# A hybrid attention/S5 layer on one core: the in-projection keeps its split weights in DRAM, and the FFN's silu becomes one ScalarE instruction

## The chip, the core and the metric

The kernel runs on one core of a Trainium2 chip. The engines that matter here are TensorE (PE: matmuls, with PEld for its weight loads), VectorE (DVE), ScalarE (ACT), GpSimd (POOL) and SyncE (SP), which issues most DMAs. Each engine works through its own instructions in order. A DMA issued by an engine stands in that engine's instruction order: if it has to wait for a buffer, everything behind it on that engine waits too. The metric is device time in microseconds (us), the median of several runs; lower is better.

## The reference, cut to what matters

One layer over 2048 latent tokens of width 1024 with 256 context tokens, all in fp32:

```python
n_lat = modulate(rmsnorm(h, attn_norm_g), sh1, sc1)          # and n_ctx of the context
q, k, v, u, gate_attn, gate_ssm = split(n_lat @ w_in)         # 512,512,512,512,1024,1024 columns
a = neighbourhood_attention(rope(q), rope(k), v, k_ctx, v_ctx, rpb)   # 8x16 window + context keys
s = s5_branch(u_ctx, u)                                       # two-way complex diagonal scan
h = h + g1 * ((sigmoid(gate_attn) * (a @ w_branch_attn) + sigmoid(gate_ssm) * (s @ w_branch_ssm)) @ w_out)
n = modulate(rmsnorm(h, ffn_norm_g), sh2, sc2)
a, b = split(n @ w_ffn_in)                                    # 2 x 2816 columns
h = h + g2 * ((silu(a) * b) @ w_ffn_out)
out = rmsnorm(h, final_norm_g)
```

## The kernel before, in words

**Three matmuls for one.** A product of fp32 numbers is made of fp32r matmuls: each operand is split in a high part (ACT cast, L70) and a low part (DVE subtract, L71), and `mm3` (L89 to L94) adds high·high, high·low and low·high in PSUM. Activations are kept split; weights are split when they are loaded.

**Weight pieces.** `piece` (L79) brings one piece of a weight matrix, 512 KB, 128 x 1024 numbers: `raw` (L73) takes one of two raw buffers and has SP load it (L76), then `split` writes `whi` and `wlo`, of which there are three buffers each. `cols` (L96) runs 24 matmuls of 512 columns with each piece (eight contraction steps, three matmuls each). `rows` (L111), for v, takes two pieces at a time, 96 matmuls of 256 columns, and both pieces are in use until the last tokens.

**The in-projection** (`in_proj`, L350) has four token blocks of 512 tokens. Each block goes through the same 28 pieces: 4 of k, 4 of v (two pairs), 4 of q (`w_qk`, `w_vu`), 16 gate pieces (`w_gate`). So each piece is loaded and split four times. Block 0 has its normalized tokens in SBUF already; blocks 1 to 3 load them at L357 (`n<-ns`) into a ring of 12 buffers. In block 1 the same ring serves `biases` (L430), which builds the attention's bias tables for eight heads on POOL: load (`n<-in_rpb`), compute (L442, L443), store (`bi<-n`, `be<-n`).

**What stands beside it.** `run` (L1211) emits the S5 scan (`s5`, L629, in sub-blocks whose tokens POOL loads at L651, `ut<-us`) first, the in-projection with a lower priority, and the attention between them; the program's scheduler merges them into one fixed order for each engine. So the pieces fill PE behind the S5's and the attention's own steps. SP's order also holds the outputs of q and k (`qs<-qt`, L368), the S5's strip loads (`mt<-strip`, L725, sixteen at a time) and its outputs (`ys<-yt`, L800).

**The FFN** (`ffn`, L1104) takes the four token blocks again. `ffn_in` makes each pair of hidden tiles with a seven-product scheme (Strassen) from weights whose sums POOL makes and which ACT and DVE split (L70, L71); DVE adds the products (L1085 to L1098). The silu of the first half is

```python
nc.scalar.activation(t, a, AF.Tanh, scale=0.5)
V.scalar_tensor_tensor(t, t, 1.0, a, op0=ALU.add, op1=ALU.mult)
```

that is, (1 + tanh(a/2))·a on ACT and DVE, and the missing factor one half is in the gate `g` (L228). Then DVE multiplies by the second half (L1137) and the result is split (`zh`, `zl`).

Of the kernel before, what the change touches and what calls it, by code (L numbers as in the profile page):

```python
# [10 lines left out]
F32 = mybir.dt.float32  # L11
F32R = mybir.dt.float32r
BF16 = mybir.dt.bfloat16
AF = mybir.ActivationFunctionType
ALU = mybir.AluOpType
# [3 lines left out]
P = 128  # L19
D = 1024  # L20
KD = D // P
# [31 lines left out]
class Kernel:  # L53
# [22 lines left out]
        self.nc.sync.dma_start(raw.rearrange("p k f -> p (k f)"), src[r, c])  # L76
        return raw

    def piece(self, src, r, c, nr):  # L79

        raw = self.raw(src, r, c, nr)
        with self.hot():
            hi = self.wh.tile([P, nr, 1024 // nr], F32R, name="whi")
            lo = self.wh.tile([P, nr, 1024 // nr], F32R, name="wlo")
            self.split(hi, lo, raw)
        next(self.between, None)
        return hi, lo

    def mm3(self, ps, l, r, first, last):  # L89

# [2 lines left out]
        mm(ps, l[0], r[1], start=False, stop=False)  # L93
        mm(ps, l[1], r[0], start=False, stop=last)  # L94

    def cols(self, pool, src, kt, c0, n, ops, tag="ps"):  # L96

        nm = 8 // kt  # L100
        for c in range(n):
            w = self.piece(src, 0, c0 + c, kt)
            for m in range(nm):
                sl = slice(m * P, (m + 1) * P)
                for i, (nt, f) in enumerate(ops):
                    ps = pool.tile([P, nt], F32, name=tag)
                    for k in range(kt):
                        self.mm3(ps, (w[0][:, k, sl], w[1][:, k, sl]), f(k), k == 0, k == kt - 1)
                    yield c * nm + m, i, ps

    def rows(self, pool, src, c, ops, tag="ps"):  # L111


        w = [self.piece(src, r, c, 4) for r in range(2)]
        for i in range(0, len(ops), 2):
            ps = pool.tile([P, 2, 256], F32, name=tag)
            for j in range(2):
                for k in range(KD):
                    self.mm3(ps[:, j], ops[i + j](k), (w[k // 4][0][:, k % 4], w[k // 4][1][:, k % 4]), k == 0, k == KD - 1)
            yield i, ps  # L120
# [6 lines left out]
    def constants(self):  # L127
        nc = self.nc
        self.cst = self.pool("cst")
        self.dr = self.pool("dr", space=DRAM)  # L130
        self.wr = self.pool("wr", 2)
        self.wh = self.pool("wh", 3)
        self.ident = self.cst.tile([P, P], F32, name="ident")
        make_identity(nc, self.ident)
        self.am = self.cst.tile([P, 92], F32, name="am")
        nc.sync.dma_start(self.am, self.I["amask"])
        self.ones = self.cst.tile([P, P], F32, name="ones")
        nc.vector.memset(self.ones, 1.0)
        self.mhalf = self.cst.tile([P, 4], F32, name="mhalf")
        nc.gpsimd.memset(self.mhalf, -0.5)  # L140
        self.hq = self.cst.tile([P, 4, NB, 4], F32, name="hq")
        d = self.dr
        self.qs = d.tile([2, 4, 2, 2, 32, L], F32, name="qs")
        self.ks = d.tile([2, 4, 2, 2, 32, LA], F32, name="ks")
        self.vs = d.tile([2, 32, 40, AW], F32, name="vs")
        self.vc = d.tile([LC, AW], F32, name="vc")
        self.bi = d.tile([H * 2, P, 440], F32, name="bi")
        self.be = d.tile([2, H * 2, P, 320], F32, name="be")
        self.us = d.tile([LA, AW], F32, name="us")
        self.ns = d.tile([NB, KD, P, 2, TB], F32, name="ns")  # L150
        self.gsc = d.tile([2, KD, NB, P, TB], F32, name="gsc")
        self.hs = d.tile([L, D], F32, name="hs")
        self.sums = d.tile([NHT, P, 2, 512], F32, name="sums")
        self.ysc = d.tile([4, P, 2, L], F32, name="ys")
        self.asc = d.tile([NB, 4, P, 2, TB], F32, name="as")
# [52 lines left out]
    def modulation2(self, tp, pp):  # L208


        nc, I = self.nc, self.I
        V = nc.vector
        for sec in (2, 3, 4, 5):
            for c2 in range(2):
                acc = tp.tile([P, 512], F32, name="macc")
                nc.gpsimd.memset(acc, 0.0)
                nc.sync.dma_start(acc[0:1], I["b_mod"][sec * D + c2 * 512:sec * D + c2 * 512 + 512].unsqueeze(0))
                for k0 in range(0, KD, 2):
                    w = self.raw(I["w_m2"], k0 // 2, (sec - 2) * 2 + c2, 2)
                    with self.hot():  # L220
                        for k in range(2):
                            V.scalar_tensor_tensor(acc, w[:, k], self.s2[:, k0 + k, 0:1], acc, op0=ALU.mult, op1=ALU.add)
                    yield
                if sec in (2, 5):
                    pg = pp.tile([P, 512], F32, name="ps")
                    nc.tensor.matmul(pg, self.ones, acc, start=True, stop=True)
                    with self.hot():
                        V.tensor_scalar(self.g[sec // 5][:, c2 * 512:c2 * 512 + 512], pg, 0.5, None, op0=ALU.mult)  # L228
                else:
                    pm = pp.tile([P, 4, 2], F32, name="ps")  # L230
                    for m in range(4):
                        nc.tensor.matmul(pm[:, m, :], acc[:, m * P:(m + 1) * P], self.ones[:, 0:2], start=True, stop=True)
                    cs = slice(c2 * 4, c2 * 4 + 4)
                    with self.hot():
                        if sec == 3:
                            V.tensor_copy(self.B[:, 2, cs], pm[:, :, 0])
                        else:
                            V.scalar_tensor_tensor(self.A[:, 2, cs], pm[:, :, 0], 1.0, self.ng[:, 1, cs], op0=ALU.add, op1=ALU.mult)
# [111 lines left out]
    def in_proj(self, ring, ev, pm, nt, nct):  # L350
        nc, I = self.nc, self.I
        V = nc.vector
        for b in range(NB):
            if b:
                nt = [ring.tile([P, 2, TB], F32R, name="n") for _ in range(KD)]
                for k in range(KD):
                    nc.sync.dma_start(nt[k].bitcast(F32), self.ns[b, k])  # L357
            t0 = b * TB
            cs = ev.tile([P, 2, TB], F32, name="cs", bufs=1)
            nc.sync.dma_start(cs, I["rope"][:, :, t0:t0 + TB])  # L360
            lat = (TB, lambda k, nt=nt: (nt[k][:, 0], nt[k][:, 1]))
# [6 lines left out]
                        nc.sync.dma_start(dst[:, j, d, h, :, t:t + n].rearrange("i r t -> r i t"), x[p:p + 32].bitcast(F32))  # L368

            def qk(c0, ops, isk):  # L370
                for jj, i, ps in self.cols(pm, I["w_qk"], KD, c0, 4, ops):
                    with self.hot():
                        qt = ev.tile([P, 2, TB], F32R, name="qt")
                        if i:
# [29 lines left out]
            for c in range(2):  # L404
                ops = [lambda k, j=j, nt=nt: tuple(nt[k][:, i, j * P:(j + 1) * P] for i in range(2)) for j in range(4)]
                if b == 0:
                    ops += [lambda k, j=j: tuple(nct[k // 2][:, k % 2, i, j * P:(j + 1) * P] for i in range(2)) for j in range(2)]
                oc = slice(c * 256, c * 256 + 256)
                for i, ps in self.rows(pm, I["w_vu"], c, ops):
                    e = ev.tile([P, 2, 256], F32, name="e")  # L410
                    with self.hot():
                        nc.scalar.copy(e, ps)
                    if i == 4:
                        nc.scalar.dma_start(self.vc[:, oc].rearrange("(j p) f -> p j f", p=P), e)
                        continue
                    row = (t0 + i * P) // 64
                    for r in range(2):
                        for hf in range(2):
                            nc.scalar.dma_start(self.vs[hf, row + r:row + 4:2, :, oc].rearrange("j c f -> c j f"),
                                              e[r * 64 + hf * 24:r * 64 + hf * 24 + 40])  # L420
            qk(0, [lat], False)
            for gi in range(2):
                for m, _, ps in self.cols(pm, I["w_gate"], KD, gi * 8, 8, [lat]):
                    g = ev.tile([P, TB], F32, name="e")
                    with self.hot():
                        nc.scalar.activation(g, ps, AF.Tanh, scale=0.5)
                    nc.scalar.dma_start(self.gsc[gi, m, b], g)
# [598 lines left out]
    def ffn_in(self, ch, b, X, pm, os, tp, up):  # L1026
# [32 lines left out]
        ops = []  # L1059
        for x in src:  # L1060
            with self.hot():
                hi = self.wh.tile([P, x.shape[1], 4, P], F32R, name="whi")
                lo = self.wh.tile([P, x.shape[1], 4, P], F32R, name="wlo")
                self.split(hi.rearrange("p a k m -> p a (k m)"), lo.rearrange("p a k m -> p a (k m)"), x)
            ops += [(hi[:, i], lo[:, i]) for i in range(x.shape[1])]
        s1, s3, s2, s4, a11, a22, a12 = ops
# [37 lines left out]
    def ffn(self, xs_, os, xp, tp, pm, first):  # L1104
        nc, I = self.nc, self.I
        V = nc.vector
        with ExitStack() as ctx:
# [13 lines left out]
            for b in range(NB):  # L1121
# [4 lines left out]
                for g, (p0, p1) in enumerate(groups):  # L1126
                    last = g == len(groups) - 1
                    zs = {}
                    for m2 in range(p0, p1):
                        ts = []  # L1130
                        for a in self.ffn_in(m2, b, X, pm, os, wp, up):
                            t = wp.tile([P, TB], F32, name="n")
                            nc.scalar.activation(t, a, AF.Tanh, scale=0.5)
                            V.scalar_tensor_tensor(t, t, 1.0, a, op0=ALU.add, op1=ALU.mult)
                            ts.append(t)
                        for m, a in enumerate(self.ffn_in(NHT // 2 + m2, b, X, pm, os, wp, up)):
                            V.tensor_tensor(ts[m], ts[m], a, op=ALU.mult)  # L1137
# [216 lines left out]
```

## Time and profile before

| | before |
|---|---|
| median of 3 runs | 3211.07 us (3209.65 to 3219.78) |
| the profiled execution's own time | 3210.19 us |
| its span in the trace | 3208.4 us |
| granted TensorE clock, mean | 0.987 |
| PE busy | 3088.2 us, 96% |
| DVE busy | 2340.6 us, 73% |
| ACT busy | 1567.5 us, 49% |
| POOL busy | 899.4 us, 28% |
| HBM read and written | 446.95 MB and 111.61 MB |

The time beside the span is what lies before and after the recorded instructions, 1.8 us. PE is busy nearly throughout, so time can be won only where PE is idle, and it is lost where something new makes it wait; the table says nothing on where that is. Block 0 of the in-projection ends at about 394 us, block 1 at 629, block 2 at 832, block 3 at 1045; the FFN begins at about 1740.

### The profile page before, as it was taken

To read this page: it belongs to the slowest core of one execution; us is meant where nothing else is said; L and a number is where in the kernel's file an instruction comes from. 1 tells how busy PE (TensorE), PEld (TensorE's weight loads), DVE (VectorE), ACT (ScalarE), POOL (GpSimd) and SP (SyncE) were. 2 spreads that over 40 slices of the span, in tenths; PEclk is the share of its full clock that TensorE was granted. 3 is DMA by queue.
4 is the path that set the end of the run, shared out by engine and by line. 5 is a ranking of instruction groups with operands and counts; after the bars stand their busy time and mean duration, and the time that the engine had idled before them with its cause. 6 is when DMAs were issued, how large, how long until landed. Compare 5 with 4: busy or idle time off the path is not lost.

```text
span 3208.4 us, 54284 instructions
## 1 busy us (share of the span) xinstructions
PE 3088.2 (96%) x20600; PEld 2716.4 (85%) x20600; DVE 2340.6 (73%) x4153; ACT 1567.5 (49%) x2746; POOL 899.4 (28%) x856
## 2 busy tenths in 40 slices
PE   7999978999999899999999999999999999999998
PEld 5988766787788788788888998989989998989988
DVE  6689787897753576665657866987868966886766
ACT  4545434454355556466554543454535543554534
POOL 2000053000223232222300544742242423341243
PEclk9999999999999999999999999999999999999999
DMA  8545467454676898887947434434434433443332
GB/s 320 187 126 170 162 195 239 170 163 143 205 242 186 268 277 241 254 250 223 267 152 248 141 122 139 148 129 134 133 128 150 135 112 125 148 145 128 116 109 102
DMA packets 212852, 564.27 MB, mean 176 GB/s; under 512 B 31784, under 2 KB 63656, under 8 KB 212592
## 3 DMA queue, kind: packets, MB, share of 16 engines
q1 hardware_dynamic: 155008, 437.48, 41.4%
q0 software_dynamic: 28032, 87.64, 10.1%
q10 hardware_dynamic: 29552, 35.70, 3.3%
q8 instruction: 162, 2.65, 0.3%
q14 instruction: 98, 0.80, 0.1%
HBM read 446.95 MB, written 111.61 MB: 174 GB/s over the span
## 4 chain that ended last, share of the span: by engine, by line
PE 74%; DVE 10%; DMA 10%; issue 3%; POOL 2%; ACT 1%; SPq 0%; ACTq 0%; POOLq 0%; DVEq 0%
PE ps L92 14%; PE ps L93 14%; PE ps L94 14%; PE ps L1075 8%; PE ps L1073 7%; PE ps L1074 7%; DVE wlo L71 3%; PE o L924 2%; DMA n<-in_rpb 2%; PE w L905 1%; PE w L884 1%; PE pv L750 1%; DMA y<-as 1%; PE c L886 1%; PE c L907 1%
## 5 line engine op out<-in xcount | busy, mean ns | idle before, releaser
L71 DVE TENSOR_TENSOR wlo<-raw,whi 128x1024 fp32r<-128x1024 f32 (+1 forms) x522 | 681.3, 1312 | 338.1 <-ACT whi L70 336.6
L70 ACT CAST whi<-raw 128x1024 fp32r<-128x1024 f32 (+1 forms) x522 | 508.1, 976 | 493.1 <-PE ps L94 184.7
L1073 PE MATMUL ps<-X,whi 128*128 128x256 f32 x2464 | 693.9, 284 | 14.0 <-DVE u L1085 8.6
L1075 PE MATMUL ps<-X,wlo 128*128 128x256 f32 x2464 | 693.3, 284 | 11.6 <-DVE wlo L71 11.5
L1074 PE MATMUL ps<-X,whi 128*128 128x256 f32 x2464 | 690.7, 283 | 0.0
L1073 PEld LDWEIGHTS ps<-X,whi 128*128 128x128 f32 x2464 | 472.0, 192 | 18.3 <-DVE u L1085 11.3
L1075 PEld LDWEIGHTS ps<-X,wlo 128*128 128x128 f32 x2464 | 471.3, 191 | 15.0 <-DVE wlo L71 14.8
L1074 PEld LDWEIGHTS ps<-X,whi 128*128 128x128 f32 x2464 | 472.0, 192 | 0.5
L92 PE MATMUL ps<-n,whi 128*128 128x512 f32 (+1 forms) x800 | 316.8, 396 | 6.9 <-ACT t L382 5.1
L94 PE MATMUL ps<-n,wlo 128*128 128x512 f32 (+1 forms) x800 | 314.8, 394 | 0.0
L93 PE MATMUL ps<-n,whi 128*128 128x512 f32 (+1 forms) x800 | 314.7, 393 | 0.0
L92 PE MATMUL ps<-whi,zh 128*128 128x512 f32 x704 | 277.1, 395 | 0.0
L94 PE MATMUL ps<-whi,zl 128*128 128x512 f32 x704 | 277.0, 394 | 0.0
L93 PE MATMUL ps<-wlo,zh 128*128 128x512 f32 x704 | 276.9, 394 | 0.0
L1056 POOL TENSOR_TENSOR os<-raw 128x512 f32<-128x512 f32 x66 | 117.4, 1779 | 396.7 <-DMA raw<-in_w_f 326.5
L70 ACT CAST whi<-os 128x1024 fp32r<-128x1024 f32 x110 | 115.4, 1049 | 208.7 <-PE ps L1074 83.9
L71 DVE TENSOR_TENSOR wlo<-os,whi 128x1024 fp32r<-128x1024 f32 x110 | 151.7, 1379 | 67.8 <-ACT whi L70 67.8
L92 PEld LDWEIGHTS ps<-n,whi 128*128 128x128 f32 x800 | 150.5, 188 | 46.0 <-ACT t L382 6.8
L93 PEld LDWEIGHTS ps<-n,whi 128*128 128x128 f32 x800 | 150.5, 188 | 34.6 <-issue 3.4
L1057 POOL TENSOR_TENSOR os<-raw,os 128x512 f32<-128x512 f32 x88 | 134.3, 1526 | 161.6 <-DMA raw<-in_w_f 159.7
L94 PEld LDWEIGHTS ps<-n,wlo 128*128 128x128 f32 x800 | 150.4, 188 | 34.1 <-issue 2.0
L92 PE MATMUL ps<-y,whi 128*128 128x512 f32 x384 | 158.4, 414 | 17.0 <-DMA y<-as 9.7
(343 smaller groups left out, 7025.3 us busy)
## 6 DMA issues: line engine op xcount, KB each, us to landing
raw<-in_w_f SPq DMA_DIRECT2D x198, 512.0 KB
raw<-sums SPq DMA_DIRECT2D x66, 512.0 KB
raw<-in_w_gate SPq DMA_DIRECT2D x64, 512.0 KB
raw<-in_w_f SPq DMA_DIRECT2D x66, 256.0 KB
raw<-in_w_qk SPq DMA_DIRECT2D x32, 512.0 KB
gsc<-e ACTq DMA_DIRECT2D x64, 256.0 KB
raw<-in_w_m SPq DMA_DIRECT2D x32, 512.0 KB
t<-gsc SPq DMA_DIRECT2D x64, 256.0 KB
```

The source lines that it names most:

```text
L70: self.nc.scalar.copy(hi, x)
L71: self.nc.vector.tensor_tensor(lo, x, hi.bitcast(F32), op=ALU.subtract)
L92: mm(ps, l[0], r[0], start=first, stop=False)
L93: mm(ps, l[0], r[1], start=False, stop=False)
L94: mm(ps, l[1], r[0], start=False, stop=last)
L750: nc.tensor.matmul(pv[g2 * 64:g2 * 64 + 64, ri, 0:SEQC], win[:, d, p, g2, ri], rhs, start=True, stop=True, skip_group_check=True)
L924: return nc.tensor.matmul(o[h, g, :, hf, :], l, r, start=(n == 0), stop=(n == nb + 1), skip_group_check=True)
L1056: nc.gpsimd.tensor_tensor(s24[:, 0], s13[:, 0], a11, op=ALU.subtract)
L1057: nc.gpsimd.tensor_tensor(s24[:, 1], a12, s24[:, 0], op=ALU.subtract)
L1073: mm(dst, a[0][:, k], xh, start=(first and k == 0), stop=False, skip_group_check=True)
L1074: mm(dst, a[0][:, k], xl, start=False, stop=False, skip_group_check=True)
L1075: mm(dst, a[1][:, k], xh, start=False, stop=(k == 3), skip_group_check=True)
```

## The change

In block 0 each piece is loaded and split as before, now into one buffer `w` with both parts, and POOL's queue then stores both parts, 1 MB, in a DRAM buffer `wk` (8, 4 and 16 pieces). In blocks 1 to 3 `piece` takes a `w` buffer and SP loads both parts into it; there is no raw buffer and no split. There are three `w` buffers of the size of the three `whi` and three `wlo`. In the FFN ACT's Silu takes the place of ACT's Tanh and the DVE instruction, and the FFN's gate is made with 1.0.

```diff
-    def piece(self, src, r, c, nr):
-
-        raw = self.raw(src, r, c, nr)
-        with self.hot():
-            hi = self.wh.tile([P, nr, 1024 // nr], F32R, name="whi")
-            lo = self.wh.tile([P, nr, 1024 // nr], F32R, name="wlo")
-            self.split(hi, lo, raw)
+    def piece(self, src, r, c, nr, kept=None, queue=None):
+        w = self.wh.tile([P, 2, nr, 1024 // nr], F32R, name="w")
+        flat = w.rearrange("p i k f -> p i (k f)").bitcast(F32)
+        if kept is not None and queue is None:
+            self.nc.sync.dma_start(flat, kept)
+        else:
+            raw = self.raw(src, r, c, nr)
+            with self.hot():
+                self.split(w[:, 0], w[:, 1], raw)
+            if kept is not None:
+                queue.dma_start(kept, flat)
         next(self.between, None)
-        return hi, lo
+        return w[:, 0], w[:, 1]
...
+        self.wk = [d.tile([n, P, 2, 1024], F32, name=f"wk{i}") for i, n in enumerate((8, 4, 16))]
...
-                        V.tensor_scalar(self.g[sec // 5][:, c2 * 512:c2 * 512 + 512], pg, 0.5, None, op0=ALU.mult)
+                        V.tensor_scalar(self.g[sec // 5][:, c2 * 512:c2 * 512 + 512], pg, 0.5 if sec == 2 else 1.0, None, op0=ALU.mult)
...
+            fill = None if b else nc.gpsimd
...
-                for jj, i, ps in self.cols(pm, I["w_qk"], KD, c0, 4, ops):
+                for jj, i, ps in self.cols(pm, I["w_qk"], KD, c0, 4, ops, kept=self.wk[0], queue=fill):
...
-                for i, ps in self.rows(pm, I["w_vu"], c, ops):
+                for i, ps in self.rows(pm, I["w_vu"], c, ops, kept=self.wk[1], queue=fill):
...
-                for m, _, ps in self.cols(pm, I["w_gate"], KD, gi * 8, 8, [lat]):
+                for m, _, ps in self.cols(pm, I["w_gate"], KD, gi * 8, 8, [lat], kept=self.wk[2], queue=fill):
...
-                            nc.scalar.activation(t, a, AF.Tanh, scale=0.5)
-                            V.scalar_tensor_tensor(t, t, 1.0, a, op0=ALU.add, op1=ALU.mult)
+                            nc.scalar.activation(t, a, AF.Silu)
```

The order of the instructions moves with it, since the scheduler places them anew. Three places are shown. Line numbers of the changed kernel are 7 or 8 higher behind the edit.

**SP, the gate pieces of block 1.** `raw` and `w` are the weight buffers, `n<-ns` is the tokens of block 2 (into ring buffers which the bias tables give back), `qs<-qt` the stored q. Before:

```order
L76 DMA raw_7336<-in_w_gate 128x1024
L368 DMA qs_78<-qt_7115 32x2x512 x4
L76 DMA raw_7370<-in_w_gate 128x1024
L357 DMA n_7812<-ns_85 128x1024
L357 DMA n_7813<-ns_85 128x1024
L76 DMA raw_7404<-in_w_gate 128x1024
L368 DMA qs_78<-qt_7161 32x2x512 x4
L76 DMA raw_7438<-in_w_gate 128x1024
L357 DMA n_7814<-ns_85 128x1024
L357 DMA n_7815<-ns_85 128x1024
```

With the change:

```order
L85 DMA w_7223<-wk2_88 128x2048
L376 DMA qs_78<-qt_7082 32x2x512 x4
L85 DMA w_7253<-wk2_88 128x2048
L376 DMA qs_78<-qt_7124 32x2x512 x2
L808 DMA ys_92<-yt_3625 256x1x1024
L376 DMA qs_78<-qt_7124 32x2x512 x2
L364 DMA n_7703<-ns_85 128x1024
L364 DMA n_7704<-ns_85 128x1024
L85 DMA w_7283<-wk2_88 128x2048
```

The first of the block-2 token loads stood behind the fourth gate piece (`raw_7370`) and stands now behind the second (`w_7253`); an S5 output (`ys`) stands ahead of it now.

**POOL, the second half of block 0.** `ut<-us` are the S5's token loads, `n<-in_rpb` is the first bias load of block 1. Before, the loads follow one another:

```order
L651 DMA ut_2878<-us_84 128x8x64
L651 DMA ut_2882<-us_84 128x8x64
L651 DMA ut_2886<-us_84 32x8x64
L651 DMA ut_3242<-us_84 128x8x64
L651 DMA ut_3246<-us_84 128x8x64
L651 DMA ut_3250<-us_84 32x8x64
L651 DMA ut_3640<-us_84 128x8x64
L436 DMA n_6572<-in_rpb 128x1x960
```

With the change stores of kept pieces (L91) stand between them:

```order
L91 DMA wk0_86<-w_5921 128x2048
L659 DMA ut_2885<-us_84 128x8x64
L91 DMA wk0_86<-w_5967 128x2048
L659 DMA ut_2889<-us_84 32x8x64
L91 DMA wk2_88<-w_6013 128x2048
L659 DMA ut_3245<-us_84 128x8x64
L91 DMA wk2_88<-w_6047 128x2048
L91 DMA wk2_88<-w_6081 128x2048
```

Each store waits for its piece's split, and the S5's loads behind it wait with it.

**DVE, the first silu of the FFN.** `wlo` is a weight's low part, `u` a Strassen sum that PE's next product waits for. Before:

```order
L71 TENSOR_TENSOR wlo_19115<-raw_19095,whi_19114 128x1024
L71 TENSOR_TENSOR wlo_19119<-raw_19097,whi_19118 128x512
L1134 SCALAR_TENSOR_TENSOR n_19089<-n_19089,n_18993 128x512
L1085 TENSOR_TENSOR u_19129<-ps_19123,u_19129 128x256
L1134 SCALAR_TENSOR_TENSOR n_19092<-n_19092,n_18994 128x512
L71 TENSOR_TENSOR wlo_19244<-os_19236,whi_19243 128x1024
```

With the change:

```order
L71 TENSOR_TENSOR w_18693<-raw_18676,w_18693 128x1024
L71 TENSOR_TENSOR w_18696<-raw_18678,w_18696 128x512
L1093 TENSOR_TENSOR u_18706<-ps_18700,u_18706 128x256
L71 TENSOR_TENSOR w_18820<-os_18813,w_18820 128x1024
L1099 TENSOR_TENSOR u_18705<-ps_18701,u_18705 128x256
```

The two L1134 are gone, and the sum `u` stands directly behind the splits. ACT has one `ACT_TABLE_LOAD` more in the whole program, ahead of its first Silu.

## Rows read from the trace of the kernel before

**Rows 1.** Windows by stage: busy us (instructions) by engine, clock, DMA, GB/s.

```profile
core 0: us, PE busy (x) PEld busy (x) DVE busy (x) ACT busy (x) POOL busy (x), PEclk, DMA share, GB/s
150.00:394.00 244.00, 242.65 (x1464) 199.73 (x1463) 194.78 (x417) 115.40 (x254) 10.59 (x13) 1.00 0.47 143
394.00:540.00 146.00, 117.85 (x647) 95.84 (x645) 124.87 (x211) 56.38 (x118) 66.16 (x67) 0.95 0.70 211
540.00:1045.00 505.00, 496.54 (x2807) 400.40 (x2808) 355.10 (x730) 244.88 (x476) 71.89 (x121) 0.99 0.61 190
1740.00:3208.00 1468.00, 1434.07 (x9920) 1333.50 (x9918) 1118.17 (x1424) 693.74 (x1077) 557.13 (x357) 0.99 0.39 132
```

**Rows 2.** Windows in the FFN: early stretch and the later one.

```profile
1790.00:2190.00 400.00, 380.77 (x2631) 352.58 (x2630) 329.29 (x393) 186.22 (x286) 207.64 (x126) 1.00 0.41 139
2190.00:3090.00 900.00, 893.64 (x6153) 831.00 (x6152) 678.95 (x890) 437.77 (x663) 285.18 (x190) 1.00 0.40 131
```

**Rows 3.** Groups by line and form, ACT: table load, first part of silu.

```profile
L1133 ACT ACTIVATE n<-n 128x512 f32<-128x512 f32 x88 | 52.1, 627 | 9.8 <-DVE n L1098 7.7 <-DVE n L1095 1.0
...
L171 ACT ACT_TABLE_LOAD x1 | 1.3, 1283 | 2.1 <-issue 2.1
```

**Rows 4.** Groups by line and form, DVE: second part of silu.

```profile
L1134 DVE SCALAR_TENSOR_TENSOR n<-n 128x512 f32<-128x512 f32 x88 | 65.5, 779 | 0.2
```

**Rows 5.** Waits of PE in the FFN: us in total, times, longest.

```profile
PE ps L1075 <- DVE wlo L71: 11.5, 14, 1.7
PE ps L1073 <- DVE u L1085: 8.6, 10, 1.6
```

**Rows 6.** DVE's timeline at such a wait: start, us, operation.

```profile
1814.97 3.46 DVE L1134 SCALAR_TENSOR_TENSOR n<-n 128x512 f32<-128x512 f32 x2
1818.36 0.41 DVE L1085 TENSOR_TENSOR u<-ps,u 128x256 f32<-128x256 f32 x1
```

**Rows 7.** Groups by line and form, 394 to 1045 us: splits.

```profile
L71 DVE TENSOR_TENSOR wlo<-raw,whi 128x1024 fp32r<-128x1024 f32 x82 | 101.3, 1235 | 76.6 <-ACT whi L70 76.1
L70 ACT CAST whi<-raw 128x1024 fp32r<-128x1024 f32 x83 | 86.9, 1047 | 81.8 <-PE ps L93 46.6 <-DMA raw<-in_w_qk 9.6 <-DMA raw<-in_w_glu 8.3
```

**Rows 8.** Waits of PE in the bias stretch, 394 to 540 us.

```profile
PE pv L750 <- DVE p L758: 8.0, 2, 6.4
PE py L780 <- DMA mt<-strip: 5.3, 1, 5.3
PE ps L92 <- ACT t L382: 3.7, 3, 2.8
PE pv L750 <- ACT win L695: 3.0, 1, 3.0
...
PE pt L694 <- DVE Lr L688: 2.1, 1, 2.1
```

**Rows 9.** Chain of waits, 394 to 560 us: start, us, what.

```profile
393.70 13.19 DMA raw<-in_w_qk
...
508.42 9.86 DMA n<-in_rpb
...
525.45 11.26 DMA bi<-n
```

**Rows 10.** SP's timeline: block 2's tokens behind the biases.

```profile
535.10 2.07 SPq L357 DMA_DIRECT2D n<-ns  x2
```

**Rows 11.** PE's timeline in block 1: two matmuls of 512 columns.

```profile
410.05 0.40 PE L92 MATMUL ps<-n,whi 128*128 128x512 f32 x1
410.29 0.39 PE L93 MATMUL ps<-n,whi 128*128 128x512 f32 x1
```

**Rows 12.** Chain of waits, 629 to 700 us: a quick piece load.

```profile
667.65 3.20 DMA raw<-in_w_qk
```

**Rows 13.** DMA in 40 slices of 74 to 114 us.

```profile
GB/s 179 301 192 274 401 442 401 422 410 389 401 373 229 324 406 360 311 217 303 401 418 347 75 63 271 1 260 2 0 287 397 397 410 401 418 274 315 205 303 258
```

**Rows 14.** DMA issues: a POOL store, KB, median us to landing.

```profile
bi<-bi POOLq DMA_DIRECT2D x16, 880.0 KB, 9.9
```

More of the change, by code (lines that the diff above doesn't have):

```diff
@@ L94, in mm3, with cols @@
         mm(ps, l[1], r[0], start=False, stop=last)
-    def cols(self, pool, src, kt, c0, n, ops, tag="ps"):
+    def cols(self, pool, src, kt, c0, n, ops, tag="ps", kept=None, queue=None):
         nm = 8 // kt
         for c in range(n):
-            w = self.piece(src, 0, c0 + c, kt)
+            w = self.piece(src, 0, c0 + c, kt, kept[c0 + c] if kept is not None else None, queue)
             for m in range(nm):
@@ L109, in cols, with rows @@
                     yield c * nm + m, i, ps
-    def rows(self, pool, src, c, ops, tag="ps"):
-        w = [self.piece(src, r, c, 4) for r in range(2)]
+    def rows(self, pool, src, c, ops, tag="ps", kept=None, queue=None):
+        w = [self.piece(src, r, c, 4, kept[c * 2 + r] if kept is not None else None, queue) for r in range(2)]
         for i in range(0, len(ops), 2):
@@ L1061, in ffn_in @@
             with self.hot():
-                hi = self.wh.tile([P, x.shape[1], 4, P], F32R, name="whi")
-                lo = self.wh.tile([P, x.shape[1], 4, P], F32R, name="wlo")
+                hl = self.wh.tile([P, 2, x.shape[1], 4, P], F32R, name="w")
+                hi, lo = hl[:, 0], hl[:, 1]
                 self.split(hi.rearrange("p a k m -> p a (k m)"), lo.rearrange("p a k m -> p a (k m)"), x)
```

## The prediction, written before the changed kernel ran

> **What bounds the kernel now.** I read the windows by stage first. PE is busy for 242.65 of 244 us in block 0 of the in-projection (150 to 394 us), 117.85 of 146 in the first part of block 1 (394 to 540), 496.54 of 505 in the rest of blocks 1 to 3 and 1434.07 of 1468 in the FFN [rows 1]. So PE sets the time; the change leaves PE's matmuls as they are, and no edit can win more in a stretch than its idle PE time: 1.4, 28.2, 8.5 and 33.9 us, 72 us in all. The question for each edit is which part of these gaps it closes, and whether it opens new ones.
>
> **The FFN.** Its idle time is not spread evenly. The 400 us from 1790 lose 19.2 us, the 900 us after them 6.4 [rows 2]; DVE is busy for 82% of the first and 75% of the second stretch. PE waits 11.5 us in 14 places for a weight's low part and 8.6 us in 10 places for the sum `u`, both from DVE [rows 5]. One such place shows how it comes about: two silu instructions take DVE 3.46 us, and the 0.41 us sum that PE waits for begins as they end [rows 6]. The change takes these 88 instructions of 779 ns, 65.5 us, out of DVE's line [rows 4], and a Silu stands on ACT where the Tanh of 627 ns stood [rows 3]; I take its cost as the same, since it reads and writes the same 128 x 512, and ACT, busy for 47% of the FFN [rows 1], has room even if it were twice that. Of the gains I count all 8.6 us of the waits for `u`, since the order puts the sum straight behind the splits, and two thirds of the 11.5, 7.7, since 65.5 us less of 1118 does not empty DVE's queue: **16 us won**. The bounds are 8.6 (only the sums) and 20.1 (all of both).
>
> **The table load.** ACT's only load of function tables now takes 1283 ns [rows 3]; one more stands ahead of the first Silu. **1.3 us lost** at most, nothing if PE has work queued there, so nothing is at stake. The Trainium skill ("ScalarE: Activation LUTs", section What ACT_TABLE_LOAD costs) counts a drain beside the load, 2.66 us for a switch of sets; by that the sum would be 1.4 us higher. No run here shows the drain.
>
> **The splits of blocks 1 to 3.** 84 subtracts on DVE (82 lie within 394 to 1045, 1235 ns each, 101.3 us) and as many casts on ACT (1047 ns, 86.9 us) go [rows 7]. What they free matters only where PE idles. In the bias stretch PE waits 8.0 us for the attention's `p` and 2.1 for `Lr`, both DVE, and 3.7 and 3.0 us for ACT [rows 8], 16.8 us in which an engine that loses splits comes last; DVE is busy for 124.87 of these 146 us and PE's clock is at 0.95 [rows 1]. I take half, **8 us won** (bounds nothing and 16.8): these are waits in chains of the scan and the attention, which are as long as their own steps, and only the queue in front of them shrinks, by about 146/651 of 101.3, 23 us of 125. In 540 to 1045 us only 8.5 us are idle; I take a quarter, **2 us won**.
>
> What does not shrink is the bias chain. The loads of the bias tables and the stores behind them follow one another on POOL until 508.42 + 9.86 and then 525.45 + 11.26 us [rows 9]; at 535.10 the tokens of block 2 get the ring buffers that this frees [rows 10], and SP holds the gate pieces behind these token loads. The order in the changed kernel puts the first of these token loads behind the second gate piece instead of the fourth, so in-projection work is held earlier, by two pieces; scan and attention work must fill PE in its place. The order has it there, so I count no loss in the likeliest case.
>
> **The direct loads.** A matmul of 512 columns starts 0.24 us after the one before [rows 11], so a piece of 24 is 5.6 us. With three buffers a load is issued when PE leaves the piece three before it, and has two pieces, 11.2 us, to land. Before, two raw buffers stood in front of the three split ones, so a load was asked for two pieces earlier. The nearest rows for landing are 512 KB: 3.20 us at a quiet place [rows 12], 13.19 us in the crowd at the start of block 1 [rows 9]. The full rate in slices of the trace is around 410 GB/s [rows 13], so the second 512 KB adds 1.3 us: 4.5 to 14.5 us against 11.2. I take the value near the lower end, since the whole of the DMA engines is not full: 394 to 1045 us stands at 0.63 (0.70 and 0.61 weighted by 146 and 505 us [rows 1]), and 84 x 1.3 us adds 107 of 651, which makes 0.79. One place is late in any case. Both pieces of a v pair are held until the pair's end, so of the next pair only one can be loaded ahead; the other is asked for at the end and takes 4.5 us, where before it was in a raw buffer and took only a split, 1.05 + 1.24 = 2.3 us [rows 7]. That is 2.2 us in each of three blocks, 6.6; a little of it lies behind other PE work: **6 us lost** (bounds nothing, if all of it does, and 40, below).
>
> **The stores of block 0.** 28 stores of 1 MB, each 2.6 us of all DMA engines, 72 us, most of it in 244 us with a share of 0.47 [rows 1], which becomes about 0.77. A store holds its buffer until it lands, about 10 us after the split by the nearest row of POOL's queue, 880 KB in 9.9 us [rows 14]; PE needs the buffer itself for about 11 us of waiting and 5.6 us of work, so the store is hidden by PE's use of the piece. If that cover is gone, the price is below. PE idles 1.4 us there now, and something will be caught in the queue: **3 us lost**.
>
> The sum: -16 - 8 - 2 + 1.3 + 6 + 3 = -15.7 us. Against the profiled execution, a span of 3208.4 us and a time of 3210.2, that gives 3194.5; the median of the runs is 0.9 above that execution, so **3195 us**.
>
> **Rivals.** *No change.* DVE's relief gives only the sums' 8.6 us, the bias chain sets block 1 as before and nothing is won there, and the in-projection loses its 6 + 3 and the table load 1.3: 3211.1 - 8.6 + 10.3 = 3213 us. For it speaks that every engine but PE is under 86% in each stage, and that the bias chain is untouched; against it that the waits name DVE and ACT, not DMA, in most of their places.
>
> *Larger gain.* All waits that name DVE or ACT go: -20.1 - 16.8 - 8.5 with the same losses, +10.3: 3211 - 35 = 3176 us. Against it: a wait's removal uncovers the next one, and the 5.3 us wait for the strip loads [rows 8] shows DMA right behind.
>
> *Slower: direct loads late.* In the busy stretches (0.70 and more with the extra bytes at 0.86) a load needs the 14.5 us of the crowded row and misses its 11.2 by 3.3. The forecast's gain is spent when five loads are late in this way and the bound of slower is passed at eight (25 / 3.3); with 12 of the 84 it is 40 us in place of 6, -15.7 + 34 = +18: 3229 us. Against it: a late load needs another one in front of it, and the loads are spaced by PE itself.
>
> *Slower: stores that hold the buffers.* If each of the 28 stores is kept back by one split on DVE (1.24 us [rows 7]) and all of that reaches PE, block 0 loses 35 us in place of 3: 3195 + 32 = 3227 us. It decides (gain spent) at half of that. Rows of before show POOL's 880 KB landing in 9.9 us [rows 14], with no way to tell what part of it is waiting. The Trainium skill ("SBUF — State Buffer", the box on the trap "DVE blocks DMA") says that DMAs issued from GpSimd's queue stall for want of descriptors while DVE runs an operation in a two-port mode, and sends them to SP's or ACT's queue. It speaks against this change's choice of queue; by it this rival is the likely case.
>
> **How the numbers follow.** A difference under 0.3%, 9.6 us, is about what a measurement of this kernel cannot tell from no change. Chances: the forecast (3184 to 3201 us) 0.42, larger gain 0.13, no change (3201 to 3221) 0.28, late loads 0.11, held stores 0.06. Faster takes the first two, 0.55; same is 0.28; slower 0.17. The forecast's own range is 3184 to 3201; cases of both signs count, so the range that holds the time 8 times in 10 goes from 3168, under the larger gain, to 3226, where the slower cases begin, since these are 0.17 and some of them lie within.
>
> **What the changed profile should show.** FFN: no wait of PE for the sum `u`, the waits for `wlo` at 4 us, PE idle under 8 us between 1790 and 2190; one table load more. 394 to 1045 us: DVE some 100 us less busy, DMA at about 0.79, PE's idle in 394 to 540 at 20 us, a wait of some 2 us per block for the second piece of the second v pair. Block 0: PE idle 4 us, DMA near 0.77. The prediction is wrong if PE waits for `w` from DMA outside the v pairs, if block 0 is over 5 us longer, if the bias chain starts later (then block 1 ends later by as much), or if the FFN's waits stay and merely name another DVE instruction.

## The result and the profile after

The changed kernel takes 3227.12 us (median of 16 runs, 3217.56 to 3237.17) against 3210.52 us (16 runs) before: a ratio of 1.0051, 95% interval 1.0037 to 1.0065. It is slower by 17 us where 3195 was forecast. The profiled execution took 3222.0 us with a span of 3220.2.

The windows by stage of the changed kernel, at the times of [rows 1] and [rows 2], with the same columns:

```profile
150.00:394.00 244.00, 243.14 (x1483) 200.93 (x1483) 191.85 (x406) 115.04 (x249) 24.15 (x38) 1.00 0.73 250
394.00:540.00 146.00, 119.38 (x637) 95.53 (x636) 120.44 (x220) 47.96 (x116) 59.41 (x63) 0.89 0.73 243
540.00:1045.00 505.00, 477.95 (x2797) 388.85 (x2796) 287.60 (x708) 195.78 (x432) 90.96 (x150) 0.98 0.79 258
1740.00:3208.00 1468.00, 1454.04 (x10049) 1352.87 (x10049) 1065.43 (x1344) 693.21 (x1079) 556.06 (x354) 1.00 0.40 134
...
1790.00:2190.00 400.00, 390.90 (x2715) 363.23 (x2715) 317.53 (x373) 190.27 (x299) 216.07 (x130) 0.99 0.42 142
```

Between 540 and 1045 us PE idles 27.1 us where it idled 8.5; in the FFN's early stretch 9.1 where it idled 19.2. Cut at the first and last matmul of the FFN the account is plain. Windows of before, then of the changed kernel:

```profile
0.00:1777.50 1777.50, 1691.62 (x11001) 1420.41 (x11002) 1240.97 (x2750) 886.73 (x1704) 349.76 (x505) 0.98 0.68 212
1777.50:3166.30 1388.80, 1363.21 (x9459) 1269.34 (x9458) 1079.99 (x1372) 668.05 (x1017) 534.60 (x340) 1.00 0.40 132
```

```profile
0.00:1803.50 1803.50, 1702.70 (x11001) 1431.89 (x11002) 1151.83 (x2666) 813.72 (x1620) 359.47 (x533) 0.97 0.77 250
1803.50:3178.20 1374.70, 1360.74 (x9459) 1268.74 (x9458) 1015.97 (x1284) 664.08 (x1017) 534.97 (x340) 1.00 0.40 134
```

The FFN is 14.1 us shorter (1388.8 to 1374.7). What lies ahead of it is 26.0 us longer: idle PE time goes from 85.9 to 100.8 us, and the same 11001 matmuls keep PE busy 11.1 us longer, at a mean granted clock of 0.97 instead of 0.98. So the silu did what it was to do, and the in-projection lost more than that. Most of it lies between 629 and 1055 us, here before and changed:

```profile
629.00:1055.00 426.00, 419.88 (x2442) 342.38 (x2442) 294.79 (x609) 207.75 (x396) 72.08 (x121) 0.99 0.64 197
629.00:1055.00 426.00, 403.43 (x2430) 334.18 (x2427) 220.63 (x548) 166.40 (x351) 83.80 (x141) 0.98 0.82 266
```

PE idles 22.6 us there instead of 6.1. Before, the longest wait of that stretch is one for a split:

```profile
PE ps L92 <- ACT whi L70: 5.2, 1, 5.2
```

PE's longest waits in blocks 1 to 3 of the changed kernel (us in total, times, longest):

```profile
PE ps L98 <- DMA w<-wk: 22.8, 6, 6.1
PE pv L758 <- DVE p L766: 5.4, 3, 3.9
PE py L789 <- DVE h L780: 4.3, 1, 4.3
PE ps L98 <- DMA n<-ns: 3.9, 2, 2.0
PE ps L98 <- ACT e L420: 3.3, 2, 1.8
```

The first row is new: PE waits for kept pieces. Of its 22.8 us 22.3 lie between 629 and 1055 us, nearly all that PE idles there. Three of the six waits lie close together. The first of these three can be read from SP's timeline and the chain of waits of the changed kernel:

```profile
755.08 0.34 SPq L85 DMA_DIRECT2D w<-wk  x1
756.42 1.91 SPq L376 DMA_DIRECT2D qs<-qt  x4
759.92 10.48 SPq L733 DMA_DIRECT2D mt<-strip  x16
770.50 1.94 SPq L376 DMA_DIRECT2D qs<-qt  x4
772.54 3.08 SPq L85 DMA_DIRECT2D w<-wk  x2
```

```profile
772.54 12.28 DMA w<-wk
...
784.96 0.76 PE ps L98
785.72 0.43 PE ps L99
786.15 0.43 PE ps L100
786.57 0.43 PE ps L98
787.00 0.43 PE ps L99
```

PE left the buffer at 763.9 us (the last matmul of the piece three before), but SP was in a burst of sixteen strip loads and issued the load only at 772.54; the piece landed 12.28 us later and PE stood for 5.4 us. And the wait has a tail: the matmuls behind it follow one another at 0.43 us, not 0.24 [rows 11], while the granted clock is at the lower of its two levels, for some 3 us. At the two waits that follow the DMA engines have no time left, as their 40 slices of 812 to 852 us show:

```profile
DMA  0299989999988999999999999999999999999999
```

There the attention's first loads (bias tables, keys, values, on POOL's queue) meet the gate pieces of block 2. The loads issued at 822.90 and 833.06 us landed after 13.7 and 18.3 us. SP's order has a share in the second of them too: PE had left its buffer at 825.6 us, 7.5 us before the issue, but a load of another stage stood ahead of it on SP and could go only at 832.64, when DVE had freed its buffer:

```profile
822.47 8.50 DMA raw<-in_w_m
...
832.64 0.33 SPq L76 DMA_DIRECT2D raw<-in_w_glu  x1
833.06 18.26 DMA w<-wk
```

### The profile page after: what moved, and what is told of

Read it like the earlier page. It is cut to its first block, busy times and chain, and to the rows that moved or that the text cites. A ratio compares the mean times of both kernels' runs of the same rounds, so it can differ in the third digit from the quotient of the medians.

```text
span 3220.2 us, 54055 instructions
## 1 busy us (share of the span) xinstructions
PE 3096.7 (96%) x20600; PEld 2727.3 (85%) x20600; DVE 2189.0 (68%) x3981; ACT 1490.7 (46%) x2663; POOL 909.1 (28%) x884
## 4 chain that ended last, share of the span: by engine, by line
PE 73%; DMA 10%; DVE 9%; POOL 3%; issue 3%; ACT 2%; SPq 0%; ACTq 0%; POOLq 0%; DVEq 0%
PE ps L98 14%; PE ps L99 13%; PE ps L100 13%; PE ps L1083 7%; PE ps L1081 7%; PE ps L1082 7%; PE o L932 2%; DVE w L71 2%; DMA w<-wk 1%; PE w L913 1%; PE w L892 1%; DMA raw<-in_w_f 1%; DMA raw<-in_w_m 1%; PE pv L758 1%; DMA raw<-in_w_bs 1%
## 5 line engine op out<-in xcount | busy, mean ns | idle before, releaser
L71 DVE TENSOR_TENSOR w<-raw,w 128x1024 fp32r<-128x1024 f32 (+1 forms) x438 | 573.8, 1317 | 288.7 <-ACT w L70 285.5
L1081 PE MATMUL ps<-X,w 128*128 128x256 f32 x2464 | 695.6, 284 | 7.5 <-DVE u L1093 3.6
L1082 PE MATMUL ps<-X,w 128*128 128x256 f32 x2464 | 693.8, 283 | 0.0
L1083 PE MATMUL ps<-X,w 128*128 128x256 f32 x2464 | 687.1, 284 | 6.5 <-DVE w L71 6.3
L70 ACT CAST w<-raw 128x1024 fp32r<-128x1024 f32 (+1 forms) x438 | 421.1, 962 | 374.1 <-PE ps L100 216.6
L1081 PEld LDWEIGHTS ps<-X,w 128*128 128x128 f32 x2464 | 472.0, 192 | 10.2 <-DVE u L1093 4.8
L1083 PEld LDWEIGHTS ps<-X,w 128*128 128x128 f32 x2464 | 466.6, 192 | 9.6 <-DVE w L71 9.6
L1082 PEld LDWEIGHTS ps<-X,w 128*128 128x128 f32 x2464 | 472.0, 192 | 0.5
L98 PE MATMUL ps<-n,w 128*128 128x512 f32 (+1 forms) x800 | 320.5, 401 | 25.5 <-DMA w<-wk 17.7
L99 PE MATMUL ps<-n,w 128*128 128x512 f32 (+1 forms) x800 | 319.5, 399 | 0.0
L100 PE MATMUL ps<-n,w 128*128 128x512 f32 (+1 forms) x800 | 318.1, 398 | 0.0
L99 PE MATMUL ps<-w,zh 128*128 128x512 f32 x704 | 277.3, 394 | 0.0
L100 PE MATMUL ps<-w,zl 128*128 128x512 f32 x704 | 277.1, 394 | 0.0
L98 PE MATMUL ps<-w,zh 128*128 128x512 f32 x704 | 276.6, 394 | 0.0
L98 PEld LDWEIGHTS ps<-n,w 128*128 128x128 f32 x800 | 153.2, 191 | 66.2 <-issue 23.6
L71 DVE TENSOR_TENSOR w<-os,w 128x1024 fp32r<-128x1024 f32 x110 | 147.7, 1343 | 78.9 <-ACT w L70 78.8
L100 PEld LDWEIGHTS ps<-n,w 128*128 128x128 f32 x800 | 153.5, 192 | 35.0 <-issue 2.0
L99 PEld LDWEIGHTS ps<-n,w 128*128 128x128 f32 x800 | 153.1, 191 | 34.2 <-issue 3.2
L98 PE MATMUL ps<-y,w 128*128 128x512 f32 x384 | 156.7, 410 | 6.6 <-ACT w L70 3.6
```

Source lines behind the costliest of these rows:

```text
L70: self.nc.scalar.copy(hi, x)
L71: self.nc.vector.tensor_tensor(lo, x, hi.bitcast(F32), op=ALU.subtract)
L98: mm(ps, l[0], r[0], start=first, stop=False)
L1081: mm(dst, a[0][:, k], xh, start=(first and k == 0), stop=False, skip_group_check=True)
L1082: mm(dst, a[0][:, k], xl, start=False, stop=False, skip_group_check=True)
L1083: mm(dst, a[1][:, k], xh, start=False, stop=(k == 3), skip_group_check=True)
```

## The experiments

Each kernel was compared with the kernel before on the same chip. "Lost" below is worked out from windows of 10 us: idle PE time, plus busy time times what the granted clock lacks to 1.00. The stages are cut at fixed times, so the work in them is not the same from kernel to kernel: the last in-projection matmul of block 3 ends at 1056 us before and at 1142 us in the changed kernel, which does scan work earlier.

| kernel | ratio to before (95%) | lost 0-150 | 394-629 | 629-1055 | 1055-1670 | FFN starts |
|---|---|---|---|---|---|---|
| before | 1 | 23.9 | 34.8 | 9.1 | 38.9 | 1777.5 |
| changed | 1.0051 (1.0037-1.0065) | 28.4 | 43.4 | 29.6 | 32.7 | 1803.5 |
| silu alone | 0.9985 (0.9974-0.9997) | 22.4 | 37.3 | 8.4 | 41.9 | 1781.7 |
| kept alone | 1.0096 (1.0077-1.0114) | 31.4 | 47.9 | 29.6 | 32.9 | 1810.4 |
| half loads | 1.0143 (1.0128-1.0158) | 29.2 | 54.4 | 29.3 | 51.1 | 1827.9 |
| half loads, six slots | 0.9952 (0.9936-0.9967) | 29.5 | 38.0 | 0.0 | 39.8 | 1769.0 |
| fourth from raw | 0.9995 (0.9982-1.0008) | 28.9 | 37.1 | 5.4 | 50.2 | 1790.4 |
| strips on POOL | 1.0039 (1.0025-1.0053) | 27.6 | 34.1 | 25.3 | 44.7 | 1794.5 |
| stores alone | 1.0054 (1.0036-1.0073) | 28.4 | 38.9 | 10.5 | 42.4 | 1798.1 |
| tiny stores | 0.9985 (0.9973-0.9996) | 26.3 | 40.0 | 10.8 | 35.9 | 1784.9 |
| gates, fourth | 1.0071 (1.0051-1.0092) | 24.3 | 38.9 | 35.1 | 43.1 | 1807.6 |
| fourth, ACT stores | 1.0018 (1.0005-1.0032) | 29.2 | 43.6 | 3.1 | 57.3 | 1798.3 |
| fourth, strips on POOL | 0.9942 (0.9929-0.9956) | 31.9 | 18.5 | 1.4 | 46.1 | 1766.1 |

Each edit of the in-projection also gives the scheduler's order another form. Between 1055 and 1670 us the kernels lose 32.7 to 57.3 us, though no wait of the changed kernel there is for a kept piece. So a difference of 20 us in the whole time is no proof of a cause by itself; the waits in the stage that the edit aims at say more.

**The two edits apart.** Before with the FFN's edit only, and the changed kernel with the old Tanh and DVE instruction.

> Only the FFN's silu is changed; PE's, SP's and POOL's instructions stand in the order of before. In the changed kernel the FFN, from its first to its last matmul, took 1374.1 us against 1388.2 before, 14.1 less. If the silu's gain is its own, this kernel takes 3210.5 - 14 = 3196 us, and the waits of PE for the sum u and for the low part fall from 8.6 and 11.5 us to about 4 and 6. If part of the FFN's gain came from the other edit (an FFN that starts at another time against its weight loads), it takes 3200 us or more.

> Only the kept pieces, with the old silu; PE's, SP's and POOL's order is that of the changed kernel. If the two edits add up, the time before the FFN grows by the 26 us of the changed kernel (first FFN matmul at 1803.5 against 1777.5 us) and the FFN stays at 1388: 3210.5 + 26 = 3237 us. If the two edits work against each other, it is under 3230.

Measured: 3201.03 us against 3208.08 of before, and 3233.89 us. The edits add up within the runs' spread (-7 and +26 for +17). PE's waits in the FFN of the silu alone:

```profile
PE ps L1075 <- DVE wlo L71: 9.0, 11, 1.6
PE ps L1073 <- DVE u L1085: 3.2, 5, 1.5
```

The waits for `u` fall as expected (8.6 to 3.2), those for the low part less (11.5 to 9.0). The FFN of its profile took 1375.3 us, 13.5 less than before; the median moved by only half of that, and with the same PE order ahead of the FFN its profile began the FFN 4 us later. How much of this is spread between executions stays open.

**Bytes or lead.** In blocks 1 to 3 only the high half is loaded, into the same three buffers, and stands in for the low half too, whose part of the result is left out:

```diff
-            self.nc.sync.dma_start(flat, kept)
+            self.nc.sync.dma_start(flat[:, 0], kept[:, 0])
+            next(self.between, None)
+            return w[:, 0], w[:, 0]
```

> Blocks 1 to 3 load only the high parts, 512 KB a piece, into the same three buffers, and use them for the low parts too: the low parts are left out of the result, PE's matmuls stay 24 a piece, and the stores stay at 1 MB. Theory, direct loads of 1 MB land late: the waits of PE for kept pieces fall from 22.8 us to under 8, and the time to 3227 - 20 = 3207 us or less. Rival, three buffers in front of PE are too few whatever the size, or SP issues the loads late: the waits stay over 15 us and the time over 3220. Rival, the stores of block 0 cost the time: over 3220 with the waits gone.

Measured: 3251.56 us, slower than the changed kernel. PE's waits for kept pieces between 629 and 1055 us are 18.1 us, where the changed kernel has 22.3, and the stage loses as much (29.3 and 29.6 us):

```profile
PE ps L100 <- DMA w<-wk: 18.1, 4, 10.3
PE ps L100 <- DMA n<-ns: 3.7, 2, 2.4
```

So the theory that a load is late because it has 1 MB fell. What makes this kernel slower still lies in the other stages (54.4 and 51.1 us lost against 43.4 and 32.7), where its order is another. The longest wait, 10.3 us, was for 512 KB that took 19 us to land in the rush of the attention's loads. A second theory took its place: the loads are asked for too late, whatever their size. The same kernel, with the same memory cut into six buffers of 512 KB:

```diff
-        self.wh = self.pool("wh", 3)
+        self.wh = self.pool("wh", 6)
...
+        hi = self.wh.tile([P, nr, 1024 // nr], F32R, name="w")
+        if kept is not None and queue is None:
+            self.nc.sync.dma_start(hi.rearrange("p k f -> p (k f)").bitcast(F32), kept[:, 0])
+            next(self.between, None)
+            return hi, hi
+        lo = self.wh.tile([P, nr, 1024 // nr], F32R, name="w")
```

> As the half loads (512 KB a piece in blocks 1 to 3, the low parts left out of the result), but the same memory is cut into six buffers of 512 KB, so that a load is asked for five pieces ahead of PE and not two. The half loads at two pieces took 3251.6 us and waited 19.4 us for kept pieces. New theory, the lead of the load is too short, whatever its size: the waits for kept pieces go (under 3 us) and the time falls by 20 us or more, to 3230 or less. Rival, the new order of the work (the scan moved ahead of the in-projection) costs the time, not the loads: it stays over 3240.

Measured: 3191.96 us, 60 under the three buffers, with no wait for a kept piece and PE busy throughout blocks 2 and 3. The same stretch of three and of six buffers, in windows:

```profile
629.00:1055.00 426.00, 404.20 (x2480) 334.93 (x2477) 228.36 (x570) 171.59 (x361) 84.74 (x142) 0.97 0.68 204
```

```profile
629.00:1055.00 426.00, 426.00 (x2679) 354.27 (x2675) 238.43 (x605) 187.94 (x391) 96.98 (x163) 1.00 0.72 219
```

The order of the work differs between the two as well, so not all of the 60 us need be the lead. What the waits show is that the 18.1 us for kept pieces are gone, with the lower clock behind them.

**A fourth buffer.** Two ways. In the first a pool of one more buffer is opened behind the scan's.

> All as in the changed kernel, with a fourth weight buffer for the in-projection, so that a load has three pieces, 16.8 us, to land, not two. Theory, direct loads land late: the waits of PE for kept pieces fall from 22.8 us to under 6, and the time to 3205 us, about that of before minus a third of the silu's gain. Rival, the stores of block 0 or the new order cost the time: 3220 us or more.

Measured: 3519.57 us, and no test of the theory: the in-projection ran no matmul of block 0 between its first pieces, at 201 us, and 642 us, where the scan ends. That the new pool lies in memory which the scan holds until then is the likely reason. The windows show a scan alone, PE busy for half of the time and DMA at 0.14:

```profile
200.00:650.00 450.00, 235.17 (x1114) 163.72 (x1113) 371.20 (x907) 178.00 (x457) 20.46 (x29) 0.62 0.14 44
```

In the second the raw buffers, idle in blocks 1 to 3, serve as the fourth:

```diff
+        if kept is not None and queue is None:
+            self.turn = getattr(self, "turn", 0) + 1
+            if self.turn % 4 == 0:
+                w = [self.wr.tile([P, nr, 1024 // nr], F32, name="raw") for _ in range(2)]
+                for i, x in enumerate(w):
+                    self.nc.sync.dma_start(x.rearrange("p k f -> p (k f)"), kept[:, i])
+                next(self.between, None)
+                return w[0].bitcast(F32R), w[1].bitcast(F32R)
```

> The changed kernel, where every fourth direct load goes into the two raw buffers (512 KB each), which blocks 1 to 3 don't need: four pieces of lead without more memory, the result whole. Theory of the short lead: the waits of PE for kept pieces fall from 22.8 us to under 10, and the time from 3227 to 3215 us or less. Rival, order or stores: 3222 us or more.

Measured: 3204.41 us, level with before; the medians put it 23 us under the changed kernel, the ratios to before, each on its own chip, 18. Between 629 and 1055 us one wait for a kept piece is left:

```profile
PE ps L106 <- DMA w<-wk: 2.8, 1, 2.8
PE ps L106 <- ACT t L398: 0.9, 1, 0.9
```

DMA was at 0.85 in that stretch, more than the 0.82 of the changed kernel. One piece more of lead, with every byte in place, and PE's waits for kept pieces fall from 22.8 us to 2.8. The order of the work differs from the changed kernel's from block 1 on, so the gain in time is not the lead's alone for certain; the waits are what shows its work.

**SP's order.** The strip loads on POOL (`nc.gpsimd.dma_start(mt[...` at L733), first without, then with the fourth buffer.

> The changed kernel with the scan's strip loads (128 issues of 16 KB, some 0.6 us each, in bursts of 10 to 19 us) on POOL's queue, not SP's. Theory, SP's order holds direct loads back: the loads that were issued 8.6 to 17.5 us after their buffer came free (behind such a burst) go out at once, the wait of 5.4 us at the gate pieces of block 2 goes, and the time falls to 3218 us or less. Rival, the full DMA engines alone make the loads late: 3225 or more.

> Both cures in one: the fourth direct load into the raw buffers (3204 us, 23 under the changed kernel) and the scan's strip loads on POOL's queue (3221, 6 under it). If the two losses are apart, in lead and in SP's order, they add up: 3227 - 23 - 6 = 3198 us, under the silu alone (3201). If both cure the same late loads, it stays at 3204.

Measured: 3220.93 and 3188.58 us. Alone it wins nothing that is clear: 1.0039 of before against 1.0051, with intervals that overlap. In 629 to 1055 us PE's wait for kept pieces is

```profile
PE ps L98 <- DMA w<-wk: 19.4, 3, 12.5
```

with 12.5 us in one place, where the attention's loads come in. The wait at 785 us is gone, as was meant, and a longer one stands 40 us behind it: that load was issued 2.8 us after its buffer came free and took 20.8 us to land. Together with the fourth buffer it is worth 16 us, and the time is below what was expected of the sum (3198). Most of those 16 us lie between 394 and 629 us (18.5 us lost instead of 37.1), not at the kept pieces of blocks 2 and 3; why, no run shows. PE's waits from 394 to 1055 us are then small and mixed:

```profile
PE pv L766 <- DVE p L774: 2.6, 1, 2.6
PE py L798 <- DVE h L788: 2.5, 1, 2.5
PE pt L811 <- DVE yn L804: 2.5, 1, 2.5
...
PE ps L106 <- DMA w<-wk: 1.0, 1, 1.0
```

This version beats both kernels: 0.9942 of before (0.9929 to 0.9956), about 19 us.

**The stores of block 0.** Stores and silu with raw loads and splits in all blocks; then the same with stores of 8 columns; then only the gate pieces kept (with the fourth buffer); then the stores on ACT's queue (with the fourth buffer).

> Silu and the stores of block 0 as in the changed kernel; blocks 1 to 3 load and split raw weights as before. The changed kernel lost 4.5 us in the first 150 us and nothing more in block 0. If that is what the stores cost: 3201 (silu alone) + 4.5 = 3206 us. Rival, the stores cost most of the loss, through buffers that they hold or transfers that they delay: 3217 us or more.

> As the stores alone, but each store writes 8 of its 1024 columns, so the 28 stores move 0.2 MB and not 29 MB; what is stored is read by nobody. The order of the work shifts again a little. The stores alone took 3224 us, the silu alone 3201. If the stored bytes cost the 23 us between them, this kernel takes 3201 to 3205 us. If only the 6 us of the first 150 us come from the bytes and the rest from the order that the scheduler found, it lies at 3210 to 3220.

> As the fourth buffer out of the raw ones (3204 us), but only the 16 gate pieces are kept; the k, v and q pieces of all blocks are loaded raw and split as before. No store then lies in the first 150 us, where the changed kernel, the stores alone and the fourth buffer lost 5 to 7 us more than before (28.4, 28.4 and 28.9 us against 23.9). If these come from the stores, they go, and the time is 3198 us or less. If they have another cause, or the raw loads of k, v and q in blocks 1 to 3 are what holds PE, it is 3204 or more.

> As the fourth buffer out of the raw ones (3204 us), with the stores of block 0 issued by ACT and not by POOL. If stores on POOL's queue are held back while DVE is busy (the Trainium skill, SBUF — State Buffer, box on the trap DVE blocks DMA), the first 150 us lose 24 us again and not 29, and the time is 3199 or less. If the loss there is the transfers' share of the DMA engines, the queue changes nothing: 3204 within 5, or more where ACT's own work waits behind a store.

Measured: 3224.26, 3203.38, 3231.81 and 3213.83 us. A price of the stores shows in the first 150 us, where the pieces of k are stored while the first tokens are loaded: 28.4 us lost with them, 24.3 where the gates alone are kept, 23.9 before. Kernels with the same stores lie between 27.6 and 31.9. The windows of the first 150 us, before and after, show DMA rise from 0.72 to 0.77 and PE's idle time from 18.6 to 21.7:

```profile
0.00:150.00 150.00, 131.44 (x1036) 114.10 (x1037) 102.18 (x369) 75.67 (x120) 24.02 (x24) 0.95 0.72 268
```

```profile
0.00:150.00 150.00, 128.28 (x986) 110.26 (x987) 99.67 (x365) 72.27 (x115) 23.61 (x27) 0.94 0.77 289
```

ACT's queue changes nothing there (29.2 against 28.9), so it is not POOL's issuing. That it is the transfers is shown in part only: with tiny stores 26.3 us are lost, between the two. The rest of the 23 us between the stores alone and the silu alone is not explained by this. With tiny stores the 23 us are gone and the time is the one expected if the bytes cost them, but the traces do not bear that out. The last in-projection matmul of block 0 ends at 394.4 us with the silu alone, 401.1 with the stores and 400.1 with tiny stores; that of block 3 at 1054.9, 1067.5 and 1068.8. So up to the end of block 3 tiny stores are as late as whole ones, and the two profiles part behind it (42.4 and 35.9 us lost from 1055 to 1670, and FFN starts 13 us apart), where no store is left and each kernel has an order of its own. What costs the 23 us stays open. The gates alone were no clean test either: k, v and q still need the raw buffers which every fourth gate piece now takes, and one wait for a split is 17.9 us long:

```profile
PE ps L106 <- ACT w L70: 18.6, 2, 17.9
PE ps L106 <- ACT e L442: 10.7, 1, 10.7
```

## Why the prediction was wrong

**The direct loads: the step that failed.** The text had the fact in hand, that "Before, two raw buffers stood in front of the three split ones, so a load was asked for two pieces earlier", and gave it no price. It then took a landing near 4.5 us out of 4.5 to 14.5 because the DMA engines were not full on the mean. The mean was right (0.79 forecast; 0.73 and 0.79 measured) and of no use: at the four waits outside the v pairs the landings were 12.3 to 18.3 us, in bursts of other loads. It also took a load to be issued when PE leaves the buffer; at these four SP issued it 4.2, 8.6, 2.9 and 7.5 us later, with other loads and stores ahead of it in SP's order. The lead itself, from the free buffer to PE's need, was 11.2 to 19.8 us, no less than the 11.2 forecast. Landing and late issue together were longer, and the four waits cost 17.7 us. The v pairs, the only lateness that the sum counted, cost 1.7 and 3.5 us, 5.1 for the 6 forecast. With the lower clock and all else, the stretch from 629 to 1055 us loses 20.5 us more than before.

Two pieces of lead were too few, and size was not the reason: half the bytes waited nearly as long (18.1 us for 22.3), with six buffers for half pieces the waits were gone, and with a fourth for whole ones 2.8 us were left. An estimate from the four loads, with their landings as they were: issued at once, three would have been in time and the fourth 2.7 us late. So SP's order has a large share; no run shows how large.

**What a wait costs.** The price of 3.3 us per late load left out the clock, as did the statement that no more than the idle time can be won in a stretch. Of the 26.0 us lost ahead of the FFN 11.1 are not idle time but the same matmuls at the lower clock. They do not all belong to the late loads. By the table and the windows, 4.0 us of the 20.5 that the stretch from 629 to 1055 us loses more are clock, and 8.0 of the 8.6 from 394 to 629, where nearly all of PE's waits name other things.

**The rivals.** The slower case by late loads gave 3229 us and a chance of 0.11; the time is right, but its twelve late loads at 3.3 us were six of up to 6.1 us and their tails. That the time came out near this rival's is partly luck: the term that it names grew by less, and the splits and the stores, which it left as forecast, came out worse. The case of held stores names a loss of 35 us in block 0; from 150 to 394 us PE idles 0.9 us.

**The splits.** This is a second step that failed. Of the 8 us to be won in 394 to 540 us nothing came: PE idles 26.6 us there where it idled 28.2, and the clock went from 0.95 to 0.89, so that 394 to 629 us lose 8.6 us more than before. The wait for `p` did shrink, from 8.0 us [rows 8] to 1.5, but others took its place, also of the changed kernel and the same stretch:

```profile
PE py L789 <- DVE h L780: 4.3, 1, 4.3
PE ps L98 <- DMA n<-ns: 3.9, 2, 2.0
...
PE py L790 <- DVE h L780: 2.6, 2, 1.4
...
PE pv L758 <- DVE p L766: 1.5, 2, 1.1
```

DVE's busy time there hardly fell (124.9 to 120.4): the scheduler moved scan work forward, and the scan's last `pv` product came at 777 us and not at 830. The bias chain ran later, its first load at 400.8 and its last at 526.3 us against 394.3 and 508.4 [rows 9], one of the signs that the forecast named for being wrong.

**The FFN.** Right in place and size by the profile: -14.1 for -16 + 1.3. The median of the silu alone moved by 7 us only, and the forecast had no wait for `u` left and 4 us for the low part. The waits for `u` and the low part went from 8.6 and 11.5 us [rows 5] to

```profile
PE ps L1083 <- DVE w L71: 6.3, 9, 1.2
PE ps L1081 <- DVE u L1093: 3.6, 6, 1.1
```

The Silu takes what the Tanh took, and the second table load is the 1283 ns expected:

```profile
L1141 ACT ACTIVATE n<-n 128x512 f32<-128x512 f32 x88 | 51.9, 628 | 5.5 <-DVE n L1106 4.8 <-DVE n L1103 0.3
...
L1141 ACT ACT_TABLE_LOAD x1 | 1.3, 1283 | 0.0
```

**The stores.** 3 us forecast; 4.5 us more are lost in the first 150 us than before, and nothing more up to 394 us. Block 0 ends 6.5 us later (402.8 for 396.3), which is past the 5 us that the forecast named as a sign. Whether 3 us was the right size is open, since the stores alone cost 23 us against the silu alone. The rule of the Trainium skill ("SBUF — State Buffer", the trap "DVE blocks DMA") did not show: POOL's stores of 1 MB landed in a median of 7.7 us, and ACT's queue brought nothing. The box speaks of DVE operations in a two-port mode, not of a busy DVE as such, and no run here shows which operations were in it.

## What to carry to other kernels

When a stage that makes data in a buffer (a split, a cast) is replaced by a load of the finished data, the input buffers in front of it go too, and with them the lead of the load; count buffers in pieces of lead before bytes, and give the freed input buffers back to the load. A mean DMA share says nothing on whether a load is in time: look for the bursts that it meets, in the order of the engine that issues it and on the DMA engines, and compare their length with the lead. Price a wait of PE with its tail at the lower clock. And where each edit moves the order of the whole program, judge it by the waits in its own stage before the whole time.

## What was not expected of the hardware

A 512 KB load took 19 us to land (half loads), and loads of 1 MB 18.3 us (changed kernel) and 20.8 us (strips on POOL), while the DMA engines were at 0.9 and above with loads of SP's and POOL's queues. After waits of 5 to 6 us PE ran at the lower clock level (0.43 us from one 512-column matmul to the next instead of 0.24) for 3 us at 785 us and 5 us at 851 us.
